# Three rearrangements in a two-layer transformer kernel: normalised softmax rows, a joined differential softmax, routing in channel order

## The chip, the cores and the metric

The kernel runs on one core of a Trainium2 chip. The time is device microseconds (us) of one execution, the median of several runs. Engines are called PE (matrix multiply), PEld (its weight load), DVE (vector), ACT (scalar), POOL and SP; DMA issues stand on ACT's or SP's queue.

## The reference, cut to what matters

256 tokens of width 1024 in float32 go through two layers of a first block and then two layers of a second block.

```python
# first block, per layer: attention of 8 GQA heads and 8 MLA heads
sc = jnp.einsum('bqhgd,bkhd->bhgqk', qblk, k).astype(jnp.float32) * scale
p = jax.nn.softmax(sc, axis=-1).astype(v.dtype)
return jnp.einsum('bhgqk,bkhd->bqhgd', p, v)
...
```

The second block modulates its two norms by a vector of a condition `c` (shift, scale and gate for each norm), mixes the tokens by a gated linear attention, a retention and a differential attention, and then sends each token to a few of 32 experts. The differential attention takes softmax(S0) - lam * softmax(S1) under a causal mask, multiplies by the values and applies a norm over each head's 128 outputs. The router computes logits = (norm(x) * g * (1 + scale) + shift) @ router_w, a sigmoid, and a group-limited choice of the top experts.

## The kernel before, in words

`first_layer(0)` and `first_layer(1)` run first, then `second_mix(0)`, `second_moe(0)`, `second_mix(1)`, `second_moe(1)`. Every engine runs its instructions in the order in which the program writes them. Weights come in 2 MB pieces through one list on SP's queue into eight slots; from a slot ACT copies a "granule" of 128x512 as the rounded high part (L257, `wh`) and DVE subtracts it to get the low part (L269, `wl`), a few granules ahead of PE, which multiplies high and low parts one after the other (all ordinary matmuls stand at L150).

**First-layer attention (`attention`, L680 to L720).** There are 16 units per layer of two (head, query tile) pairs each. One turn `i` of the loop issues: scores of unit i on PE; copies of finished transposes `PTs`; `soft` for unit i-1 (DVE row maximum L667, two ACT exponentials L670 that also give the row sums `su`); `soft_diag` for unit i-2 (L673: a DVE reciprocal, then two 128x128 diagonal matrices of it through `diag`, L428 to L431, one on DVE and one on POOL); `fill(i)`, which multiplies other weights' granules; and for unit i-3 four matmuls of P with the diagonal (L718), which turn and scale P at once. Each of them is two instructions on PE.

```python
                    mm(PT[h][:, o:o + 128], P[:, j, kt * 128:(kt + 1) * 128], dg[j], True, True)
```

**Differential attention (in `second_mix`).** Eight units (4 heads, 2 query tiles) per layer; tile 0 sees 128 keys, tile 1 sees 256. `d_soft` (L1532) makes two exponentials, `d_diag` (L1540) a reciprocal, a multiplication by -lam and two diagonals, and PE adds P0 diag(1/s0) and P1 diag(-lam/s1) into one bank for each key tile. `head_norm` (L1192) then takes the norm of each head.

**The modulation vector turned (`turn_mod`, L374).** The shift and scale of the second norm (columns 24:40 of `modc`, channel k*128+p on partition p) are needed with channel p*8+k on partition p (`modr`). ACT's queue writes them to a DRAM tensor `mod_turned`, element by element, at the start of `second_mix(0)` (L1243), between the loads of the constants `c` (L1226) and `GB` (L1242); they are read back behind the H projection (L1263). On ACT the squares of x (`sumsq`, L406) for the first norm of the mix come behind these issues; POOL makes the reciprocal root (L483, L414, L415), and ACT and DVE scale x (`DA`), which PE turns (L454).

**Routing (in `second_moe`, L1676 to L1783).** x is turned on PE with a stride of eight channels (`turn`, L1688), so that channel p*8+k lies on partition p; a bias matmul of the shift with `router` follows; the logits are made with the scaled router `ra` as the 32-column stationary operand in four column groups, copied by DVE (`lg`), summed over the groups and turned back by a matmul with `sumI`. `warm` then issues 20 matmuls whose result is not used. DVE adds the bias (`th`), ACT takes a tanh (L1734), a chain of some twenty DVE instructions picks experts, PE counts tokens (`sel`), and `place` multiplies one-hot rows `oh` with the normed tokens `xr`. The MoE follows, which streams expert weights.

Of the kernel before, what the change touches and what calls it, by code (L numbers as in the profile page):

```python
# [67 lines left out]
def constants():  # L68
# [20 lines left out]
    for lv in range(7):  # L89
# [27 lines left out]
       ("kv_a_norm_g", 2), ("b_gate", 16), ("norm1_g_2", 8), ("b_mod_2", 48),  # L117
# [17 lines left out]
def build(ctx, tc, I, out, cols, cols2, dbg=None):  # L135
# [537 lines left out]
    def soft_diag(P, su):  # L673
        r = small(2)
        dve.reciprocal(r, su)
        return P, [diag(r[:, j:j + 1], pool if j else dve) for j in range(2)]

    def attention(n, qk, heads_of, pair, vsrc, fill):


        Sb, PD, PT, full_, PS, cnt = {}, {}, {}, [], {}, {}
        for i in range(n + 4):
            if i < n:
                Sb[i] = qk(i)
# [12 lines left out]
            if 0 <= i - 2 < n:  # L697
                PD[i - 2] = soft_diag(*PD[i - 2])
# [12 lines left out]
            P, dg = PD.pop(u)  # L711
# [480 lines left out]
    def head_norm(src, g, e, gate, dest):  # L1192
# [3 lines left out]
        def squares():  # L1196
            sq, ss = t2((128, g * e), name="sq"), small(g)
            act.activation(sq, src, AF.Square)
            dve.tensor_reduce(ss, sq.rearrange("p (g e) -> p g e", e=e), axis=AX.X, op=OP.add)
            hold["r"] = rstd(ss, e)  # L1200
# [21 lines left out]
    def second_mix(l):  # L1222
# [4 lines left out]
        if l == 0:  # L1227
            turn_mod(False)
# [34 lines left out]
        if l == 0:  # L1263
            turn_mod(True)
# [32 lines left out]
        act.activation(GB[:, 512:1024], ob, AF.Copy)  # L1297

# [59 lines left out]
        for _ in proj("D1_%d" % l, qk_evac(0)):  # L1358
            pass

# [171 lines left out]
        def d_soft(v, n):  # L1532
            nm, su, r = small(2), small(2), small(2)
            dve.tensor_reduce(nm, v, axis=AX.X, op=OP.max, negate=True)
            P = t2((128, 2, 256), name="P")
            for j in range(2):
                act.activation(P[:, j, :n], v[:, j], AF.Exp, bias=nm[:, j:j + 1], accum_out=su[:, j:j + 1])
            return P, su, r

        def d_diag(P, su, r):  # L1540
            dve.reciprocal(r, su)
            dve.tensor_tensor(r[:, 1:2], r[:, 1:2], neglam[l], op=OP.mult)
            return P, [diag(r[:, j:j + 1], pool if j else dve) for j in range(2)]

        def d_norm(pr):
            return head_norm(oD.pop(0), 4, 128, gsub[l][:, None, None, :].to_broadcast([128, 2, 2, 128]),
                             mixed[:, :, 256 + pr * 256:512 + pr * 256])
        nu = len(units)
        turned = None
        for i in range(nu + 4):  # L1550
# [8 lines left out]
            if 0 <= i - 2 < nu:  # L1559
                PD[i - 2] = d_diag(*PD[i - 2])  # L1560
            if 0 <= i - 1 < nu:
                PD[i - 1] = d_soft(Sb.pop(i - 1), 128 * (units[i - 1][1] + 1))
# [21 lines left out]
            P, dg2 = PD.pop(i - 3)  # L1584
            if t == 0:
                AT[h] = bank()
            for kt in range(t + 1):
                b = AT[h][:, (kt + t) * 128:(kt + t + 1) * 128]
                for j in range(2):
                    mm(b, P[:, j, kt * 128:(kt + 1) * 128], dg2[j], j == 0, j == 1)  # L1590
# [31 lines left out]
        a2 = small(8, name="a2")  # L1622
        ra = t2((128, 8, NE), name="ra")
        dve.scalar_tensor_tensor(a2, modr[:, l, 1], 1.0, g2run[:, l], op0=OP.add, op1=OP.mult)
        pool.tensor_tensor(ra, router, a2[:, :, None].to_broadcast([128, 8, NE]), op=OP.mult)
# [51 lines left out]
    def second_moe(l):  # L1677
# [5 lines left out]
        def turn(k0, on_act):  # L1683
            p = bank()
            for k in (k0, k0 + 1):
                for t in range(2):
                    o = (k - k0) * 256 + t * 128
                    pe.transpose(p[:, o:o + 128], x[:, t, k::8], ident)  # L1688
# [3 lines left out]
            else:  # L1692
                dve.tensor_copy(xT[k0 // 2], v)
        steps[0]()
# [7 lines left out]
        dve.tensor_copy(rb, p[:, :NE])  # L1702
# [3 lines left out]
        turn(4, False)  # L1706
        turn(6, True)


        xr = [[wk.tile([128, 4, 128], F, name="xr", tag=("macc", "wh")[h], bufs=(NACC, NSPLIT)[h]) for h in range(2)] for t in range(2)]  # L1710
        for h in range(2):
            for t in range(2):
                act.activation(xr[t][h], x[:, t].rearrange("p (c k) -> p k c", k=8)[:, h * 4:h * 4 + 4], AF.Copy, scale=rx[:, t:t + 1])  # L1713
# [12 lines left out]
        for t in range(2):  # L1726
            mm(p[:, t * 32:(t + 1) * 32], lg[:, t * 128:(t + 1) * 128], sumI, t == 0, True)
# [6 lines left out]
        act.activation(th, th, AF.Tanh, scale=0.5)  # L1734
        dve.scalar_tensor_tensor(bi.rearrange("p (t e) -> p t e", t=2), th.rearrange("p (t e) -> p t e", t=2), 0.5,
# [333 lines left out]
```

## Time and profile before

| | before |
|---|---|
| median of 3 runs | 2126.85 us (2126.64 to 2130.85) |
| the profiled execution | 2126.68 us, span 2124.9 us |
| granted PE clock, mean | 0.976 of full speed |
| PE busy | 2024.3 us (95%) |
| DVE busy | 1011.0 us (48%) |
| ACT busy | 792.0 us (37%) |
| POOL busy | 247.9 us (12%) |

The span is the time from the first instruction to the last; the rest of the execution lies around it. A busy share is an average over stages with different limits, so a stage is read by its own stretch of time.

### The profile page before, as it was taken

To read this page: it belongs to the slowest core of one execution; us is meant where nothing else is said; L and a number is where in the kernel's file an instruction comes from. 1 tells how busy PE (TensorE), PEld (TensorE's weight loads), DVE (VectorE), ACT (ScalarE), POOL (GpSimd) and SP (SyncE) were. 2 spreads that over 40 slices of the span, in tenths; PEclk is the share of its full clock that TensorE was granted. 3 is DMA by queue.
4 is the path that set the end of the run, shared out by engine and by line. 5 is a ranking of instruction groups with operands and counts; after the bars stand their busy time and mean duration, and the time that the engine had idled before them with its cause. 6 is when DMAs were issued, how large, how long until landed. Compare 5 with 4: busy or idle time off the path is not lost. (4 is left out here: it accounts for less than half of the span.)

```text
span 2124.9 us, 29291 instructions
## 1 busy us (share of the span) xinstructions
PE 2024.3 (95%) x11522; PEld 1382.3 (65%) x11522; DVE 1011.0 (48%) x1901; ACT 792.0 (37%) x1605; POOL 247.9 (12%) x309
## 2 busy tenths in 40 slices
PE   8999999999999997999999889998999999969998
PEld 6888999788889986686444434446686444434443
DVE  4777877777778874875111111124875111101112
ACT  6655655566565555453111111114453111101111
POOL 1211000021100002621000000003531000000000
PEclk9999999999999998999999989999999999989999
DMA  6545777454558844446999999996256999979997
GB/s 232 212 160 198 279 280 276 170 191 149 206 212 316 308 158 80 157 185 248 417 428 427 426 370 428 427 417 237 81 186 240 419 427 427 428 297 429 426 427 309
DMA packets 135472, 620.92 MB, mean 292 GB/s; under 512 B 13594, under 2 KB 18724, under 8 KB 109220
## 3 DMA queue, kind: packets, MB, share of 16 engines
q1 hardware_dynamic: 129508, 614.78, 73.1%
q10 hardware_dynamic: 5824, 4.23, 1.1%
q8 instruction: 92, 1.51, 0.3%
q14 instruction: 48, 0.39, 0.1%
HBM read 617.93 MB, written 1.06 MB: 291 GB/s over the span
## 5 line engine op out<-in xcount | busy, mean ns | idle before, releaser
L150 PE MATMUL bank<-U,wh 128*128 128x256 f32 x1536 | 287.4, 288 | 0.5 <-DVE U L440 0.4
L150 PEld LDWEIGHTS bank<-U,wh 128*128 128x128 f32 x1536 | 239.8, 190 | 8.4 <-issue 5.3
L150 PE MATMUL bank<-w_eg,qwh 128*64 128x512 f32 x1024 | 228.1, 598 | 16.5 <-issue 16.5
L150 PE MATMUL bank<-w_ed,uT 128*64 128x512 f32 x1024 | 226.8, 595 | 0.3
L150 PE MATMUL bank<-w_eu,qwh 128*64 128x512 f32 x1024 | 226.7, 595 | 0.0
L150 PE MATMUL bank<-U,wl 128*128 128x256 f32 x768 | 218.4, 284 | 4.8 <-DVE wl L269 4.8
L1823 ACT ACTIVATE qwh<-bank,modr,a 128x128 f32<-128x128 f32 x128 | 58.6, 458 | 350.1 <-PE bank L150 319.2
L150 PEld LDWEIGHTS bank<-w_eg,qwh 128*64 128x64 f32 x1024 | 73.8, 138 | 163.8 <-issue 161.0
L150 PE MATMUL bank<-wh,H 128*128 128x512 f32 x512 | 163.8, 395 | 0.0
L150 PEld LDWEIGHTS bank<-w_eu,qwh 128*64 128x64 f32 x1024 | 70.8, 137 | 139.6 <-issue 138.7
L150 PE MATMUL bank<-wh,HT 128*128 128x512 f32 (+1 forms) x448 | 156.3, 403 | 0.6 <-ACT wh L257 0.6
L150 PEld LDWEIGHTS bank<-w_ed,uT 128*64 128x64 f32 x1024 | 70.7, 137 | 129.1 <-issue 127.3
L150 PEld LDWEIGHTS bank<-U,wl 128*128 128x128 f32 x768 | 145.9, 190 | 6.1 <-DVE wl L269 6.0
L150 PEld LDWEIGHTS bank<-oh,xr 128*128 128x128 f32 x1056 | 123.2, 192 | 26.0 <-issue 24.3
L150 PE MATMUL bank<-oh,xr 128*128 128x128 f32 (+1 forms) x1056 | 131.5, 278 | 1.2 <-DVE oh L1801 1.2
L596 DVE SCALAR_TENSOR_TENSOR macc<-w_mod,cact,macc 128x512 f32<-128x512 f32 x168 | 127.0, 756 | 0.0
L440 DVE SCALAR_TENSOR_TENSOR qwl<-bank,sm,qwl 128x512 fp32r<-128x512 f32 x60 | 45.0, 751 | 170.2 <-ACT qwl L439 166.2
L1803 POOL TENSOR_TENSOR ohg<-oh,wgt 128x256 f32<-128x256 f32 x32 | 19.7, 615 | 844.0 <-DVE oh L1801 844.0
L150 PEld LDWEIGHTS bank<-wh,H 128*128 128x128 f32 x512 | 96.5, 188 | 21.7
L257 ACT ACTIVATE wh<-w_dn 128x512 fp32r<-128x512 f32 x128 | 80.8, 631 | 74.7 <-PE bank L150 71.5
L1821 DVE TENSOR_SCALAR qwh<-bank,a,modr 128x128 f32<-128x128 f32 x128 | 52.4, 410 | 117.7 <-ACT qwh L1823 117.7
L257 ACT ACTIVATE wh<-w_up 128x512 fp32r<-128x512 f32 x128 | 80.3, 630 | 73.2 <-PE bank L150 66.6
(526 smaller groups left out, 3484.0 us busy)
## 6 DMA issues: line engine op xcount, KB each, us to landing
w_eg<-in_w_gate SPq DMA_DIRECT2D x60, 2048.0 KB
w_eu<-in_w_up SPq DMA_DIRECT2D x60, 2048.0 KB
w_ed<-in_w_down SPq DMA_DIRECT2D x60, 2048.0 KB
w_mod<-in_w_mod SPq DMA_DIRECT2D x24, 2048.0 KB
w_up<-in_w_ffn_up SPq DMA_DIRECT2D x16, 2048.0 KB
w_dn<-in_w_ffn_down SPq DMA_DIRECT2D x16, 2048.0 KB
w_gate<-in_w_in SPq DMA_DIRECT2D x8, 2048.0 KB
w_D<-in_w_in SPq DMA_DIRECT2D x6, 2048.0 KB
```

The lines of the kernel that those rows point to most:

```text
L150: pe.matmul(o, a, b, start=start, stop=stop, skip_group_check=True)
L257: act.activation(hi[:, :n], src, AF.Copy)
L440: dve.scalar_tensor_tensor(lo, src, scale, hi.bitcast(F), op0=OP.mult, op1=OP.subtract)
L596: dve.scalar_tensor_tensor(acc, w[:, k], cact[:, k:k + 1], acc, op0=OP.mult, op1=OP.add)
L1803: pool.tensor_tensor(og, oh, wg3[:, :, A][:, :, :, None].to_broadcast([128, 2, 2, 64]), op=OP.mult)
L1821: dve.tensor_scalar(hg[k], o, a2[:, k:k + 1], b2[:, k:k + 1], op0=OP.mult, op1=OP.add)
L1823: act.activation(hg[k], o, AF.Identity, scale=a2[:, k:k + 1], bias=b2[:, k:k + 1])
```

## The change

1. In the first-layer attention the rows of P are multiplied by their reciprocal sums in place: the first of a unit's pair on DVE (128x256), the second on ACT (128x256). PE then only turns P, one transpose per 128x128 tile. The diagonals on DVE and POOL go.
2. In the differential attention `d_join` forms P0 - lam (s0/s1) P1 in one DVE instruction, and PE turns one tile instead of adding two products. The missing factor 1/s0 is taken up by the norm: `head_norm` gets the sums s0 and multiplies its epsilon by their square, which takes five small POOL instructions instead of two.
3. `turn_mod` turns the columns on PE, copies the 16 rows on ACT and writes rows of 512 bytes. The write moves behind the G projection, the read-back behind the first D projection.
4. Routing uses channels in natural order: x is turned from contiguous columns, the bias matmul takes the shift straight from `modc`, and the logits come directly as tokens x 32 experts (turned x stationary, `ra` moving, 32 columns), so `lg` and the sum over groups go. `router` is loaded in pieces of 128 bytes instead of 1 KB; one small DVE instruction (`an`) and one more vector load (`norm2_g_2`) come in. The four `xr` copies move behind the tanh.

```diff
-            else:
-                act.dma_start(turned_[l].rearrange("s (k p) -> p s k", p=128), modc[l][:, 24:40].rearrange("p (s k) -> p s k", s=2))
+                continue
+            p = bank()
+            pe.transpose(p[:16, :128], modc[l][:, 24:40], ident)
+            row = wk.tile([16, 128], F, name="mrow", tag="dg", bufs=6)
+            act.activation(row, p[:16, :128], AF.Copy)
+            act.dma_start(turned_[l].rearrange("s (k p) -> (s k) p", p=128), row)
...
-    def soft_diag(P, su):
+    def soft_norm(P, su):
         r = small(2)
         dve.reciprocal(r, su)
-        return P, [diag(r[:, j:j + 1], pool if j else dve) for j in range(2)]
+        dve.tensor_scalar(P[:, 0], P[:, 0], r[:, 0:1], None, op0=OP.mult)
+        act.activation(P[:, 1], P[:, 1], AF.Copy, scale=r[:, 1:2])
+        return P
...
-                    mm(PT[h][:, o:o + 128], P[:, j, kt * 128:(kt + 1) * 128], dg[j], True, True)
+                    pe.transpose(PT[h][:, o:o + 128], P[:, j, kt * 128:(kt + 1) * 128], ident)
...
-        nc.sync.dma_start(router, rows_of(I["router_w_2"]))
+        nc.sync.dma_start(router, kp(I["router_w_2"]))
...
+            ee, r = small(g), small(g)
+            pool.tensor_tensor(ee, over, over, op=OP.mult)
+            pool.tensor_scalar(ee, ee, EPS, None, op0=OP.mult)
+            pool.tensor_scalar(r, ss, 1.0 / e, None, op0=OP.mult)
+            pool.tensor_tensor(r, r, ee, op=OP.add)
+            pool.tensor_tensor(r, r, mhalf[:, :g], op=OP.pow)
...
-        def d_diag(P, su, r):
-            dve.reciprocal(r, su)
-            dve.tensor_tensor(r[:, 1:2], r[:, 1:2], neglam[l], op=OP.mult)
-            return P, [diag(r[:, j:j + 1], pool if j else dve) for j in range(2)]
+        def d_join(P, su0, su1, n):
+            r = small(1)
+            dve.reciprocal(r, su1)
+            dve.scalar_tensor_tensor(r, r, neglam[l], su0, op0=OP.mult, op1=OP.mult)
+            dve.scalar_tensor_tensor(P[:, 0, :n], P[:, 1, :n], r, P[:, 0, :n], op0=OP.mult, op1=OP.add)
+            return P
...
-                for j in range(2):
-                    mm(b, P[:, j, kt * 128:(kt + 1) * 128], dg2[j], j == 0, j == 1)
+                pe.transpose(b, P[:, 0, kt * 128:(kt + 1) * 128], ident)
...
-                    pe.transpose(p[:, o:o + 128], x[:, t, k::8], ident)
+                    pe.transpose(p[:, o:o + 128], x_chunk(t, k), ident)
...
+        def logits(k):
+            for t in range(2):
+                mm(lo_[:, t * 32:(t + 1) * 32], xT[k // 2][:, k % 2, t * 128:(t + 1) * 128], ra[:, k], k == 0 and t == 0, k == 7)
...
-            mm(p[:, :NE], b2[:, k:k + 1].to_broadcast([128, 128]), router[:, k], k == 0, k == 7)
+            mm(p[:, :NE], ms(3)[:, k:k + 1].to_broadcast([128, 128]), router[:, k], k == 0, k == 7)
...
-        p = bank()
-        for k in range(8):
-            c = (k % 4) * 32
-            mm(p[c:c + 32, :256], ra[:, k], xT[k // 2][:, k % 2], k < 4, k >= 4)
-        lg = t2((128, 256), name="lg")
-        dve.tensor_copy(lg, p[:, :256])
-        p = bank()
-        for t in range(2):
-            mm(p[:, t * 32:(t + 1) * 32], lg[:, t * 128:(t + 1) * 128], sumI, t == 0, True)
+        p = lo_
         warm(WARM)
```

Three places show how the instructions move; the rows are the programs' own order on one engine.

ACT, around the start of `second_mix(0)`, before: the loads of the constants `c` and `GB`, the two writes of `mod_turned`, and the squares of x (into `junk`).

```order
L257 ACTIVATE wh<-w_H_8219 128x272 x3
L406 ACTIVATE junk,sm<-bank 128x512 x2
L1226 DMA c_8572<-in_cst 128x2182
L380 DMA mod_turned<-modc_82 128x16x1
L380 DMA mod_turned<-modc_83 128x16x1
L1242 DMA GB<-in_m 128x896
L406 ACTIVATE junk,sm<-x 128x512 x4
L257 ACTIVATE wh<-w_H_8219 128x272
L505 ACTIVATE DA<-x,sm 128x512 x2
```

ACT behind the G projection, changed:

```order
L257 ACTIVATE wh<-w_D_0_8476 128x512 x3
L1309 ACTIVATE GB<-bank 128x256
L1311 ACTIVATE GB<-bank 128x512
L383 ACTIVATE mrow<-bank 16x128
L384 DMA mod_turned<-mrow 16x128
L383 ACTIVATE mrow<-bank 16x128
L384 DMA mod_turned<-mrow 16x128
L1322 ACTIVATE ab<-zt 128x256
```

Nothing stands any more between the load of `c` and that of `GB`, and so before the squares of x; two small copies and two writes stand behind the evacuation of G.

ACT in the middle of the first layer's attention, before (`w_ba` is the weight of branch a, `A` and `PTs` are copies of banks):

```order
L257 ACTIVATE wh<-w_ba_1178 128x512
L670 ACTIVATE P,sm<-bank,sm 128x256 x2
L934 ACTIVATE A_1444<-bank 96x512
L689 ACTIVATE PTs<-bank 128x512
L257 ACTIVATE wh<-w_ba_1178 128x512
L670 ACTIVATE P,sm<-bank,sm 128x256 x2
```

The same stretch, changed:

```order
L257 ACTIVATE wh<-w_ba_1176 128x512
L674 ACTIVATE P,sm<-bank,sm 128x256 x2
L682 ACTIVATE P<-P,sm 128x256
L941 ACTIVATE A_1432<-bank 96x512
L696 ACTIVATE PTs<-bank 128x512
L257 ACTIVATE wh<-w_ba_1176 128x512
L674 ACTIVATE P,sm<-bank,sm 128x256 x2
```

One multiplication of a 128x256 tile stands behind each pair of exponentials.

PE in the routing, before, from the last matmul of the out-projection to the placing:

```order
L150 MATMUL bank<-wh,MT 128x512
L1688 MATMUL bank<-C,x 128x128 x8
L150 MATMUL bank<-router,modr 128x32 x8
L1688 MATMUL bank<-C,x 128x128 x8
L150 MATMUL bank<-xT,ra 32x256 x8
L150 MATMUL bank<-C,lg 128x32 x2
L150 MATMUL bank<-C 128x128 x20
L150 MATMUL bank<-sel,C 128x64
```

And changed:

```order
L150 MATMUL bank<-wh,MT 128x512
L1712 MATMUL bank<-C,x 128x128 x8
L150 MATMUL bank<-router,modc_82 128x32 x8
L150 MATMUL bank<-ra,xT 128x32 x8
L1712 MATMUL bank<-C,x 128x128 x8
L150 MATMUL bank<-ra,xT 128x32 x8
L150 MATMUL bank<-C 128x128 x20
L150 MATMUL bank<-sel,C 128x64
```

Half of the logits now stand between the two groups of transposes, and the step over `lg` is gone.

## Rows read from the trace of the kernel before

**Rows 1.** The page, busy time of each engine over the span.
```profile
PE 2024.3 (95%) x11522; PEld 1382.3 (65%) x11522; DVE 1011.0 (48%) x1901; ACT 792.0 (37%) x1605; POOL 247.9 (12%) x309
```
**Rows 2.** Windows: stretch, length, then PE, PEld, DVE, ACT, POOL busy; clock; DMA share; GB/s.
```profile
91.00:153.00 62.00, 62.00 (x456) 53.64 (x456) 43.38 (x91) 37.30 (x107) 10.33 (x14) 1.00 0.44 158
488.00:551.00 63.00, 63.00 (x474) 55.23 (x472) 44.21 (x96) 36.02 (x104) 10.80 (x15) 1.00 0.38 134
1550.00:1570.00 20.00, 19.84 (x99) 15.13 (x98) 18.40 (x49) 9.78 (x34) 5.60 (x7) 1.00 0.08 28
```
**Rows 3.** Timeline of PE, first layer: start, length, instruction, count; [idle before].
```profile
83.54 1.03 PE L908 MATMUL bank<-C,T 128*128 128x128 f32 x8
...
106.93 1.05 PE L150 MATMUL bank<-dg,P 128*128 128x128 f32 x8
107.82 1.02 PE L150 MATMUL bank<-kbd,M 128*128 128x512 f32 x2
```
**Rows 4.** Groups of instructions: count, busy us, mean ns of one, idle before.
```profile
L150 PE MATMUL bank<-dg,P 128*128 128x128 f32 x352 | 48.1, 278 | 0.0
L430 DVE TENSOR_SCALAR dg<-C,sm 128x128 f32<-128x128 f32 x48 | 13.6, 283 | 1.1
L437 DVE TENSOR_TENSOR Y<-bank,Y 128x256 fp32r<-128x256 f32 x16 | 6.6, 424 | 17.3 <-ACT Y L436 17.1
L470 ACT ACTIVATE HT<-h 128x256 fp32r<-128x256 f32 x16 | 5.7, 405 | 0.0
L667 DVE TENSOR_REDUCE sm<-bank 128x2 f32<-128x512 f32 x32 | 21.8, 681 | 0.0
```
**Rows 5.** Timeline, start of the second block's first mix (ACTq is ACT's queue).
```profile
792.22 6.93 ACTq L380 DMA_DIRECT2D mod_turned<-modc  x1
...
793.86 2.74 DVE L557 SCALAR_TENSOR_TENSOR x<-ag,sm,x 128x512 f32<-128x512 f32 x4 [1.18 <-POOL sm L553]
...
799.18 4.27 ACTq L1242 DMA_DIRECT2D GB<-in_m  x1
...
806.61 0.19 POOL L483 TENSOR_TENSOR sm<-sm 128x2 f32<-128x2 f32 x1 [12.78 <-ACT junk L406]
...
808.67 1.97 PE L454 MATMUL bank<-C,DA 128*128 128x128 f32 x8 [15.85 <-ACT DA L505]
```
**Rows 6.** DMA view of 799 to 806 us: queue, packets, MB, share of 16 engines.
```profile
q10 hardware_dynamic: 3698, 0.04, 81.6%
```
**Rows 7.** Timeline, start of the second block's second mix.
```profile
1448.85 0.37 ACTq L1242 DMA_DIRECT2D GB<-in_m  x1
1449.55 2.47 DVE L1862 TENSOR_TENSOR x<-x,bank 128x512 f32<-128x512 f32 x4
...
1453.33 0.19 POOL L483 TENSOR_TENSOR sm<-sm 128x2 f32<-128x2 f32 x1 [17.35 <-ACT junk L406]
```
**Rows 8.** Timeline, routing of the first second-block layer.
```profile
959.92 3.00 POOL L1638 TENSOR_TENSOR x<-x,pn 128x512 f32<-128x512 f32 x2 [10.42 <-DVE pn L1637]
...
962.85 0.40 PE L150 MATMUL bank<-wh,MT 128*128 128x512 f32 x1
...
966.34 3.02 PE L150 MATMUL bank<-router,modr 128*128 128x32 f32 x16
...
969.17 1.95 PE L1688 MATMUL bank<-C,x 128*128 128x128 f32 x8
...
974.03 4.71 PE L150 MATMUL bank<-C 128*128 128x128 f32 x40
...
976.10 0.25 ACT L1734 ACTIVATE th<-th 128x64 f32<-128x64 f32 x1
...
980.55 1.05 PE L150 MATMUL bank<-sel,C 128*128 128x64 f32 x8 [1.81 <-DVE sel L1771]
```
**Rows 9.** Windows of both routings, columns as in rows 2.
```profile
967.00:973.50 6.50, 5.98 (x36) 4.40 (x35) 1.31 (x3) 3.85 (x8) 1.09 (x3) 0.50 1.01 429
...
1615.40:1625.60 10.20, 9.65 (x53) 8.07 (x53) 3.00 (x14) 6.46 (x10) 1.38 (x4) 0.50 0.66 280
```
**Rows 10.** Timeline, the unused matmuls in the second routing.
```profile
1622.10 6.37 PE L150 MATMUL bank<-C 128*128 128x128 f32 x40
```

More of the change, by code (lines that the diff above doesn't have):

```diff
@@ L1199, in squares @@
             dve.tensor_reduce(ss, sq.rearrange("p (g e) -> p g e", e=e), axis=AX.X, op=OP.add)
-            hold["r"] = rstd(ss, e)
+            if over is None:
+                hold["r"] = rstd(ss, e)
+                return
+            ee, r = small(g), small(g)
[4 more added lines that the diff above has]
+            pool.tensor_tensor(r, r, mhalf[:, :g], op=OP.pow)
+            hold["r"] = r
         def norm():
@@ L1359, in second_mix @@
             pass
+        if l == 0:
+            turn_mod(True)
         GA = slot("GA", [128, 4096])
@@ L1530, in d_scores, with d_soft @@
             return v
-        def d_soft(v, n):
-            nm, su, r = small(2), small(2), small(2)
+        def d_soft(v, n, first_sum):
+            nm, su = small(2), small(1)
             dve.tensor_reduce(nm, v, axis=AX.X, op=OP.max, negate=True)
             P = t2((128, 2, 256), name="P")
-            for j in range(2):
-                act.activation(P[:, j, :n], v[:, j], AF.Exp, bias=nm[:, j:j + 1], accum_out=su[:, j:j + 1])
-            return P, su, r
-        def d_diag(P, su, r):
-            dve.reciprocal(r, su)
-            dve.tensor_tensor(r[:, 1:2], r[:, 1:2], neglam[l], op=OP.mult)
-            return P, [diag(r[:, j:j + 1], pool if j else dve) for j in range(2)]
+            for j, s_ in enumerate((first_sum, su)):
+                act.activation(P[:, j, :n], v[:, j], AF.Exp, bias=nm[:, j:j + 1], accum_out=s_)
+            return P, first_sum, su, n
+        def d_join(P, su0, su1, n):
[4 more added lines that the diff above has]
+            return P
         def d_norm(pr):
             return head_norm(oD.pop(0), 4, 128, gsub[l][:, None, None, :].to_broadcast([128, 2, 2, 128]),
-                             mixed[:, :, 256 + pr * 256:512 + pr * 256])
+                             mixed[:, :, 256 + pr * 256:512 + pr * 256], sums[pr])
         nu = len(units)
+        sums = [small(4) for _ in range(2)]
         turned = None
@@ L1559, in second_mix @@
             if 0 <= i - 2 < nu:
-                PD[i - 2] = d_diag(*PD[i - 2])
+                PD[i - 2] = d_join(*PD[i - 2])
             if 0 <= i - 1 < nu:
-                PD[i - 1] = d_soft(Sb.pop(i - 1), 128 * (units[i - 1][1] + 1))
+                h1, t1 = units[i - 1]
+                j1 = t1 * 2 + h1 % 2
+                PD[i - 1] = d_soft(Sb.pop(i - 1), 128 * (t1 + 1), sums[h1 // 2][:, j1:j1 + 1])
             if i in RET_T:
@@ L1621, in second_mix @@
         g1 = bcast_row(ms(2))
-        a2 = small(8, name="a2")
+        a2, an = small(8, name="a2"), small(8, name="an")
         ra = t2((128, 8, NE), name="ra")
         dve.scalar_tensor_tensor(a2, modr[:, l, 1], 1.0, g2run[:, l], op0=OP.add, op1=OP.mult)
-        pool.tensor_tensor(ra, router, a2[:, :, None].to_broadcast([128, 8, NE]), op=OP.mult)
+        dve.scalar_tensor_tensor(an, ms(4), 1.0, V(l, "norm2_g_2"), op0=OP.add, op1=OP.mult)
+        pool.tensor_tensor(ra, router, an[:, :, None].to_broadcast([128, 8, NE]), op=OP.mult)
         route_ahead[l] = (a2, modr[:, l, 0], ra)
@@ L1693, in turn @@
                 dve.tensor_copy(xT[k0 // 2], v)
+        lo_ = bank()
+        def logits(k):
+            for t in range(2):
+                mm(lo_[:, t * 32:(t + 1) * 32], xT[k // 2][:, k % 2, t * 128:(t + 1) * 128], ra[:, k], k == 0 and t == 0, k == 7)
         steps[0]()
@@ L1699, in second_moe @@
         for k in range(8):
-            mm(p[:, :NE], b2[:, k:k + 1].to_broadcast([128, 128]), router[:, k], k == 0, k == 7)
+            mm(p[:, :NE], ms(3)[:, k:k + 1].to_broadcast([128, 128]), router[:, k], k == 0, k == 7)
         rb = small(32, name="rb")
-        dve.tensor_copy(rb, p[:, :NE])
+        for k in range(4):
+            logits(k)
+        turn(4, False)
+        turn(6, False)
         steps[2]()
@@ L1705, in second_moe @@
         rx = steps[4]()
[L1706 to L1711, printed above, removed]
-            for t in range(2):
-                act.activation(xr[t][h], x[:, t].rearrange("p (c k) -> p k c", k=8)[:, h * 4:h * 4 + 4], AF.Copy, scale=rx[:, t:t + 1])
+        for k in range(4, 8):
+            logits(k)
+        dve.tensor_copy(rb, p[:, :NE])
         def quarter(tag, dt=F):
             return wk.tile([128, 512], dt, name="q" + tag, tag=tag, bufs=NSPLIT)
-        p = bank()
-        for k in range(8):
-            c = (k % 4) * 32
-            mm(p[c:c + 32, :256], ra[:, k], xT[k // 2][:, k % 2], k < 4, k >= 4)
-        lg = t2((128, 256), name="lg")
-        dve.tensor_copy(lg, p[:, :256])
-        p = bank()
-        for t in range(2):
-            mm(p[:, t * 32:(t + 1) * 32], lg[:, t * 128:(t + 1) * 128], sumI, t == 0, True)
+        p = lo_
         warm(WARM)
@@ L1734, in second_moe @@
         act.activation(th, th, AF.Tanh, scale=0.5)
+        xr = [[wk.tile([128, 4, 128], F, name="xr", tag=("macc", "wh")[h], bufs=(NACC, NSPLIT)[h]) for h in range(2)] for t in range(2)]
+        for h in range(2):
+            for t in range(2):
+                act.activation(xr[t][h], x[:, t].rearrange("p (c k) -> p k c", k=8)[:, h * 4:h * 4 + 4], AF.Copy, scale=rx[:, t:t + 1])
         dve.scalar_tensor_tensor(bi.rearrange("p (t e) -> p t e", t=2), th.rearrange("p (t e) -> p t e", t=2), 0.5,
```

17 lines of the change are left out of this document (7 added, 10 removed).

## Prediction

> **What bounds the kernel now.** The page's first part comes first [rows 1]: PE is busy 95% of the span and no other engine over half of it. That share is a mean over stages, so the windows view is read next for the stages that the change touches [rows 2]. In both layers' attention PE is busy for all of the 62 and 63 us, while DVE has 43 to 44 us of work and ACT 36 to 37: PE sets the pace, and an instruction taken from it shortens the stage as long as the others stay under it. In the differential attention PE has 19.84 us of 20, but DVE has 18.40: PE leads by little. Two places are read from the timeline instead, since PE stands still there: the start of the second block, where PE idles 15.85 us [rows 5], and the routing, where a chain through DVE and ACT sets the end [rows 8].
>
> **First-layer attention.** Eight PE instructions of the diagonal product hold PE from 106.93 to 107.82, 0.111 us each [rows 3]. (The group's mean of 278 ns [rows 4] contains the overlap with the next instruction and is not used.) A row of eight transposes lasts 1.03 us against 1.05 [rows 3], so a transpose costs the same 0.111 us, but is one instruction where the product was two. A unit has four tiles: 8 x 0.111 - 4 x 0.111 = 0.44 us less, and 32 units give 14.2 us. What comes in lies on other engines. DVE gives up a 128x128 diagonal of 0.283 us and takes a 128x256 multiplication, bounded by 0.283 and twice that; its nearest row is 0.424 for another 128x256 operation, with two tensor inputs. That is at most 0.28 us per unit, 4.5 us per layer if at its dearest. ACT takes a 128x256 copy with a scale, 0.405 us by the nearest row, 6.5 us per layer [rows 4]. PE's 62 us shrink by some 7, to 55, with ACT at about 44 and DVE at 45 to 48: both still fit under it. On average the cover is thinner than before, and the turn's two ends are not average: ACT's multiplication waits for DVE's reciprocal, which stands behind a row maximum of 0.681 us. I take **-13**, with -7 (half swallowed) and -14.2 as bounds, -13 being near the end that the windows' free time speaks for. POOL's diagonals go as well; they were not on the path.
>
> **Differential attention.** Before, 96 PE instructions over both layers (352 of that group less 32 x 8 in the first block) cost 96 x 0.111 = 10.7 us; now 24 transposes cost 2.7. That is 8.0 us less on PE. DVE gets no lighter: the small multiplication and the 0.283 us diagonal give way to a small instruction and one of 128 or 256 columns, up to 0.424. With DVE at 18.40 of 20 us [rows 2], PE can give back little more than 1.4 us of such a stretch before DVE leads, and two such stretches per layer stand against 4.0 us. Between them I take **-6**, bounds -3 and -8. The norm behind it has one more link on its path (the two on the sums alone can run before): the step between two small POOL starts is about 0.3 us by my estimate from POOL's 0.19 us instruction [rows 5] with its wait, so **+0.6** for two layers, bounds 0 and +1.2.
>
> **Start of the second block.** Here x is done at 796.60 (793.86 + 2.74), yet POOL gets the squares' sums only at 806.61, 10.01 us later; ACT's queue is held 6.93 us by the second write of the modulation and 4.27 us by the load behind it [rows 5]. In the second layer's mix, without the writes, that load takes 0.37 us to issue, x is done at 1452.02 and POOL starts at 1453.33, 1.31 us later [rows 7]. The difference, 8.7 us, is what the two writes cost; PE has nothing else there. In the stretch from 799 to 806 the queue with these writes made 3698 packets for 0.04 MB and took 81.6% of the DMA engines' time [rows 6]. The Trainium skill ("DMA: Bandwidth & Descriptors", Rules for kernel authors) says that a last dimension that isn't contiguous becomes one descriptor per element; the packets of the trace agree, 11 bytes each. Behind G come two transposes, two copies of 16x128 (under 0.405 us each) and two issues (0.37 each), under 1.6 us on ACT beside PE's projection: I charge 0.5. So **-8.2**, bounds 0 (the wait moves behind G) and -8.7. The read-back has the whole of D1 and the attention before `a2` needs it.
>
> **Routing.** The last out-projection matmul ends at 963.25; the tanh starts at 976.10 and the count of tokens at 980.55 [rows 8]. The clock is the question: from 967 to 973.5 it was 0.50, the lower level (1.2 GHz), and in the second layer 0.50 for 10.2 us [rows 9]. At that level the 16 bias instructions took 3.02 us, 0.19 each, and 8 transposes 1.95 [rows 8]; the logits now have the bias's form, 32 instructions. The first two turns read only the first 512 columns of x, which POOL finishes at 962.92, so they start at once. Then at the lower level: turns 1.0 (still fast), bias 3.0, half of the logits 3.0, turns 2.0, two DVE copies of 128x512 at the 0.681 of another such bank read [rows 4], 1.4, logits 3.0: 976.7; half of these logits need only the first copy, so about 975.5. The bias addition follows, and the tanh starts at about 976.0, as before. At the higher level every PE term halves: turns 0.9, bias 1.8, logits 1.8, turns 0.9, copies 0.9, logits 1.8, to 971.3; tanh at 971.8, 4.3 us earlier. The unused matmuls stand ahead of the count: 4.71 us, or 6.37 in the slow stretch of the second layer [rows 8, 10]; with logits at 975.5 they end between 980.2 and 981.9, so the count could be 1.3 us later than now. PE has fewer holes than before between 963 and 967, which should hold the clock a little longer, so I take -1 per layer, **-2**, with bounds +2.6 and -8.6. The Trainium skill ("TensorE: Matmul & The Clock Gate", Part 4) says that transposes don't count as PE work for the clock in the way matmuls do, which speaks against a routing that begins with them; by it the lower level stays, which is what I forecast, and no row here separates the transposes from the gaps around them.
>
> **Small things.** The four `xr` copies behind the tanh run beside DVE's chain of 4.45 us (976.10 to 980.55 [rows 8]) and the placing starts behind the count, so they are taken as nothing. The router in 128-byte pieces is loaded at the start of the kernel among constants; 0 to +1 us, taken as nothing. Ahead of the routing the DMA engines stand at a share of 0.08 [rows 2], with nothing to fill, so what is gained ahead of the MoE is carried to the end.
>
> **Sum.** -13 - 6 + 0.6 - 8.2 - 2 = -28.6 us on the profiled 2126.68, which is 0.17 below the median of 2126.85: **2098 us**.
>
> **Rivals.**
> - *The clock holds in the routing.* For it: PE is fed without a gap from 963.25. Against: it was at 0.50 for most of this work in both layers [rows 9]. Then -8.6 replaces -2: 2091.5 us.
> - *DVE and ACT set the pace of the attentions.* For it: DVE's 18.40 of 20 us, and the new link from DVE's reciprocal to ACT and on to PE [rows 2]. Against: a third of ACT's and DVE's time is free in the first-layer stretches. Half of the PE savings arrive, -7 and -3: 2107 us.
> - *The start of the second block keeps its gap* (the change doesn't do there what it says): another transfer on ACT's queue, `c` or `GB`, holds the squares. For it: `GB` too took 4.27 us [rows 5]. Against: 0.37 in the other layer [rows 7]. Without the 8.2: 2106 us.
> - *Slower: ACT stalls in every unit.* ACT's multiplication of unit i-2 waits for the reciprocal behind DVE's row maximum and a low part, and ACT's granule copies for PE are queued behind it. The price is 32 times the stall; from 0.9 us per unit it eats the whole 28.6. A stall of a maximum and a multiplication (0.681 + 0.424 [rows 4]) gives 35: 2133 us. Against: the reciprocal's sums are a whole turn old, and 16 units share some 62 us, nearly 4 us each.
>
> **How the numbers follow.** The forecast has a chance of 0.5 with its own range 2093 to 2103; the clock that holds 0.17; half savings 0.22; the gap that stays 0.06; the stall 0.03; and 0.02 for a change that ends within 0.2% (about 4 us, what a measurement can tell from none). If all terms fell to one end together, the sum would be -39.5 or -6.2, each less likely than any case above; the range takes the cases without the stall, and some us on either side: **2086 to 2111 us**. Faster by over 0.2%: 0.95; within: 0.02; slower: 0.03.
>
> **What would show it.** In the profile after: the group of products with a diagonal gone, PE's part of the first-layer stretches shorter by some 7 us per layer, DVE and ACT still under it (right), or PE with idle time before transposes or granules, released by DVE or ACT (the second rival). At the start of the second block POOL's sum about 1.3 us behind x, and the writes' issue short. In the routing the granted clock, the length of the unused matmuls and the distance from the last out-projection matmul to the count, 17.3 us before. The prediction is wrong if the first block's share of the gain is under 7 us, or if the second block's stages grow.

## The result

The changed kernel takes 2104.05 us (median of 4 runs, 2103.31 to 2105.73), the kernel before 2126.74 (4 runs): a ratio of 0.9892, 95% interval 0.988 to 0.9905, so about 23 us less (20 to 25.5). That is faster, inside the range, 6 us short of the forecast of 2098. The profiled execution took 2105.73 us, its span 2103.9.

The page of the changed kernel, busy time of each engine, against [rows 1]:

```profile
PE 2010.9 (96%) x11348; PEld 1368.0 (65%) x11348; DVE 1014.5 (48%) x1903; ACT 803.3 (38%) x1637; POOL 218.5 (10%) x273
```

PE has 13.4 us less to do, ACT 11.3 more, POOL 29.4 less. Where the time went is read from the starts of the same instructions in both timelines (the first row ends at ACT's first copy of an FFN granule in the second layer of the first block; a routing begins with the last out-projection matmul):

| from, to | before | after | difference |
|---|---|---|---|
| first product with P, to the first FFN granule of the second layer | 486.7 | 475.1 | -11.6 |
| to PE's first turn of x in the second block | 219.7 | 211.5 | -8.2 |
| first mix, to the last out-projection matmul | 154.2 | 155.7 | +1.5 |
| first routing, to the first expert's matmul | 23.6 | 20.9 | -2.7 |
| first MoE, to PE's first turn of x in the second mix | 469.3 | 469.7 | +0.4 |
| second mix | 155.2 | 155.5 | +0.3 |
| second routing | 23.3 | 22.5 | -0.8 |
| second MoE, to the last instruction | 490.6 | 490.7 | +0.1 |

The rows add up to -21.0, the difference of the two spans.

**First-layer attention.** Timeline of PE (start, length, instruction, count; in brackets idle time and who ended it), against [rows 3], and a row some 30 us later:

```profile
106.44 0.60 PE L725 MATMUL bank<-C,P 128*128 128x128 f32 x4
106.88 1.02 PE L150 MATMUL bank<-kbd,M 128*128 128x512 f32 x2
...
140.31 1.08 PE L150 MATMUL bank<-PTs,Z 128*64 128x256 f32 x6 [0.67 <-ACT PTs L696]
```

The four transposes hold PE 0.44 us (106.44 to 106.88), the eight instructions before held it 0.89: the saving of a unit is the predicted one. The third row is new: PE waits for the copy of the turned tiles on ACT. Summed over the stretch from the first to the last product with P (each instruction counted up to the start of the next), the tiles cost PE 7.5 us less in each layer, and the products with `PTs` 1.9 us more: 0.67 of it is this one wait, 1.2 that the products stretch. The windows (columns as in [rows 2]) show how much thinner the cover is:

```profile
91.00:147.00 56.00, 55.33 (x398) 47.23 (x397) 42.26 (x89) 40.05 (x114) 0.00 (x0) 1.00 0.48 175
...
1529.00:1549.00 20.00, 17.44 (x77) 12.45 (x75) 18.61 (x45) 8.46 (x29) 2.96 (x4) 1.00 0.10 39
```

ACT has 40.05 us of work in 56, where it had 37.30 in 62. The groups name the new instructions' prices, 505 ns on ACT and 353 on DVE, and 419 for the join:

```profile
L682 ACT ACTIVATE P<-P,sm 128x256 f32<-128x256 f32 x32 | 16.2, 505 | 0.7 <-DVE sm L680 0.7
...
L681 DVE TENSOR_SCALAR P<-P,sm 128x256 f32<-128x256 f32 x32 | 11.3, 353 | 1.1
...
L1563 DVE SCALAR_TENSOR_TENSOR P<-P,sm 128x128 f32<-128x128 f32 (+1 forms) x16 | 6.7, 419 | 0.6
```

**Differential attention.** In the second of the windows above PE is down from 19.84 to 17.44 us, but DVE is busy 18.61 of 20. The whole stretch, from the start of the first product with P to the end of the last one, stands in the next windows: both layers of the changed kernel, then the second layer of the kernel before (the first is equal to it):

```profile
890.70:914.01 23.31, 20.41 (x95) 14.84 (x93) 20.27 (x49) 12.03 (x37) 4.42 (x7) 0.93 0.30 110
1537.54:1560.15 22.61, 19.22 (x95) 13.82 (x93) 20.30 (x49) 11.90 (x37) 4.43 (x7) 1.00 0.33 118
...
1558.13:1580.99 22.86, 22.70 (x131) 18.08 (x129) 19.89 (x50) 11.30 (x35) 7.41 (x10) 1.00 0.35 122
```

The stretch is as long as it was, 23.3 and 22.6 us against 22.9. PE, which had 0.2 us of idle time in it, now has 2.9 and 3.4. In the first layer the granted clock also fell to the lower level behind PE's longest wait, which the mean of 0.93 shows; in the second, with the same wait, it did not, and the difference is 0.7 us. In the kernels with the joined tile that ran, the clock fell in 14 of 18 such stretches, in those with the diagonals in none of 10. PE's new waits, from its timeline:

```profile
1544.07 0.91 PE L150 MATMUL bank<-DA,aT 128*128 128x128 f32 x6 [1.95 <-DVE sm L1561]
...
1546.12 0.63 PE L1523 MATMUL bank<-C,rt 128*128 128x128 f32 x4 [0.61 <-ACT P L1555]
...
1549.88 0.63 PE L1523 MATMUL bank<-C,rt 128*128 128x128 f32 x4 [0.66 <-DVE bank L1547]
```

**Start of the second block.** Timeline, against [rows 5]:

```profile
780.76 0.47 ACTq L1258 DMA_DIRECT2D GB<-in_m  x1
...
782.90 2.74 DVE L561 SCALAR_TENSOR_TENSOR x<-ag,sm,x 128x512 f32<-128x512 f32 x4 [1.19 <-POOL sm L557]
...
786.81 0.19 POOL L487 TENSOR_TENSOR sm<-sm 128x2 f32<-128x2 f32 x1 [3.94 <-ACT junk L410]
788.87 1.54 PE L458 MATMUL bank<-C,DA 128*128 128x128 f32 x6 [7.01 <-ACT DA L509]
```

x is done at 785.64 and POOL starts 1.17 us later, 10.01 before; PE's idle time at its first turn is 7.0 us instead of 15.85.

**Routing.** Timeline of the first layer, against [rows 8]:

```profile
944.54 0.39 PE L150 MATMUL bank<-wh,MT 128*128 128x512 f32 x1
...
945.64 1.87 PE L150 MATMUL bank<-router,modc 128*128 128x32 f32 x16
...
947.34 1.95 PE L150 MATMUL bank<-ra,xT 128*128 128x32 f32 x16
...
950.55 3.62 PE L150 MATMUL bank<-ra,xT 128*128 128x32 f32 x16
...
953.98 5.95 PE L150 MATMUL bank<-C 128*128 128x128 f32 x40
954.27 0.41 DVE L1753 SCALAR_TENSOR_TENSOR th<-bank,sm,rb 128x32 f32<-128x32 f32 x2 [2.96 <-PE bank L150]
954.72 0.26 ACT L1754 ACTIVATE th<-th 128x64 f32<-128x64 f32 x1 [6.87 <-DVE th L1753]
...
959.77 0.98 PE L150 MATMUL bank<-sel,C 128*128 128x64 f32 x8
```

The first half of the logits takes 1.95 us, the second 3.62: the clock has fallen. The unused matmuls take 5.95 and end at the token count (L150 `sel`), which therefore starts 5.05 us behind the tanh instead of 4.45. The windows:

```profile
944.50:948.50 4.00, 4.00 (x37) 3.87 (x35) 2.45 (x4) 3.14 (x8) 0.49 (x4) 1.00 1.00 356
948.50:955.00 6.50, 6.45 (x37) 6.04 (x37) 1.89 (x5) 0.28 (x2) 0.69 (x1) 0.60 0.99 411
```

PE was busy without a gap ahead of this fall, with transposes and 32-column matmuls.

### The profile page after: what moved, and what is told of

Same layout as the page of the kernel before. It is cut to its first block, busy times and chain, and to the rows that moved or that the text cites. A ratio compares the mean times of both kernels' runs of the same rounds, so it can differ in the third digit from the quotient of the medians.

```text
span 2103.9 us, 28881 instructions
## 1 busy us (share of the span) xinstructions
PE 2010.9 (96%) x11348; PEld 1368.0 (65%) x11348; DVE 1014.5 (48%) x1903; ACT 803.3 (38%) x1637; POOL 218.5 (10%) x273
## 5 line engine op out<-in xcount | busy, mean ns | idle before, releaser
L150 PE MATMUL bank<-U,wh 128*128 128x256 f32 x1536 | 288.0, 289 | 0.3
L150 PEld LDWEIGHTS bank<-U,wh 128*128 128x128 f32 x1536 | 240.2, 190 | 8.2 <-issue 5.0
L150 PE MATMUL bank<-w_eg,qwh 128*64 128x512 f32 x1024 | 228.2, 599 | 16.7 <-DMA w_ed<-in_w_down 16.3
L150 PE MATMUL bank<-w_ed,uT 128*64 128x512 f32 x1024 | 226.8, 595 | 0.3
L150 PE MATMUL bank<-w_eu,qwh 128*64 128x512 f32 x1024 | 226.7, 595 | 0.0
L150 PE MATMUL bank<-U,wl 128*128 128x256 f32 x768 | 218.7, 285 | 4.8 <-DVE wl L269 4.7
L150 PEld LDWEIGHTS bank<-w_eg,qwh 128*64 128x64 f32 x1024 | 73.8, 138 | 164.1 <-issue 161.2
L150 PE MATMUL bank<-wh,H 128*128 128x512 f32 x512 | 163.9, 395 | 0.0
L150 PEld LDWEIGHTS bank<-w_eu,qwh 128*64 128x64 f32 x1024 | 70.8, 137 | 139.6 <-issue 138.6
L150 PE MATMUL bank<-wh,HT 128*128 128x512 f32 (+1 forms) x448 | 156.9, 404 | 0.6 <-ACT wh L257 0.6
L150 PEld LDWEIGHTS bank<-w_ed,uT 128*64 128x64 f32 x1024 | 70.7, 137 | 129.1 <-issue 127.3
L150 PEld LDWEIGHTS bank<-U,wl 128*128 128x128 f32 x768 | 146.0, 190 | 6.1 <-DVE wl L269 6.0
L150 PEld LDWEIGHTS bank<-oh,xr 128*128 128x128 f32 x1056 | 123.1, 192 | 25.8 <-issue 24.3
L150 PE MATMUL bank<-oh,xr 128*128 128x128 f32 (+1 forms) x1056 | 131.4, 278 | 0.9 <-DVE oh L1826 0.8
L150 PEld LDWEIGHTS bank<-wh,H 128*128 128x128 f32 x512 | 96.5, 188 | 21.7
```

Of the source, the lines that this page charges most:

```text
L150: pe.matmul(o, a, b, start=start, stop=stop, skip_group_check=True)
```

## The experiments

**Each part alone on the kernel before.** Four kernels take one part of the diff each: the normalised rows (`soft_norm` and its transposes), `turn_mod` with its two new places, `d_join` with the norm's epsilon, and the routing with the router's load. Here and below, a ratio is against runs of the kernel before that were made beside it.

```diff
+        dve.tensor_scalar(P[:, 0], P[:, 0], r[:, 0:1], None, op0=OP.mult)
+        act.activation(P[:, 1], P[:, 1], AF.Copy, scale=r[:, 1:2])
```

> The kernel before with the first-layer attention alone changed (rows of P multiplied by the reciprocal sums, transposes in place of the diagonal product). Theory A (PE gives up 7.1 and 7.5 us in the two layers, and about 1.9 us of each comes back as PE waiting for the PTs copies): 11 to 12 us less than before, about 0.9945 of it. Theory B (the sum of the prediction, nearly all of the 14.2 arrives): 13 us less or more.

```diff
+            act.dma_start(turned_[l].rearrange("s (k p) -> (s k) p", p=128), row)
```

> The kernel before with the turning of the modulation alone changed (rows of 512 bytes, written behind the G projection, read back behind D1). Theory A (the element writes cost only the wait at the start of the second block): 8.2 us less, POOL's first sum of that mix about 1.3 us behind x. Rival (the writes' wait moves behind G): the gain is below 5 us, and PE idles behind the G projection.

```diff
+            dve.scalar_tensor_tensor(P[:, 0, :n], P[:, 1, :n], r, P[:, 0, :n], op0=OP.mult, op1=OP.add)
```

> The kernel before with the differential attention alone changed (one joined tile, one transpose for each key tile, the sums in the norm's epsilon). Theory A (DVE sets the pace there, and the join is a dearer DVE instruction than the diagonal): 0 to 2 us slower than before, PE with some 4 us of idle time per layer in that stretch, released by DVE. Theory B (PE sets the pace, as the prediction had it in part): 6 us faster.

```diff
+                mm(lo_[:, t * 32:(t + 1) * 32], xT[k // 2][:, k % 2, t * 128:(t + 1) * 128], ra[:, k], k == 0 and t == 0, k == 7)
```

> The kernel before with the routing alone changed (natural channel order, logits straight, the router's load in small pieces). Theory A (the clock falls to the lower level in the second half of the logits and the unused matmuls hold the token count): 2 to 4 us faster in all. Rival (the whole chain is shorter by the tanh's advance): 4 to 9 us faster. Rival (the router's load in 128-byte pieces delays the first weights): a later start of the first projection, up to 1 us lost.

Measured against 2128.15 us of the kernel before in these runs:

| part | median | ratio (95%) | us |
|---|---|---|---|
| normalised rows | 2116.67 | 0.9948 (0.9933 to 0.9962) | -11.1 |
| modulation by rows | 2120.09 | 0.9957 (0.9944 to 0.997) | -9.1 |
| joined differential softmax | 2128.31 | 1.0003 (0.9994 to 1.0012) | +0.6 |
| routing | 2121.91 | 0.9965 (0.9952 to 0.9978) | -7.4 |

The four add up to -27.0, the whole measured -22.7; each part's interval reaches 2 to 3 us to either side, which covers the difference of 4 us. Three of the six runs of the normalised rows took 2113 us and three 2120 to 2121, so their median lies between two groups; by the timeline, PE's first turn of x in the second block comes 11.7 us earlier behind the first product with P, which supports the -11.1.

The first three came out as theory A had it; PE's idle time in the joined stretch was 3.4 and 2.9 us of the 4 expected. The routing came out as the second theory, more than the profiles of before and after show together (-3.5). Of the third, the first product with P starts at 101.8 to 102.3 us in the five kernels with the old load of the router and at 101.8 to 103.8 in the nine with the new one: some 0.6 us on the mean, which stays open. The two layers of the routing's one profiled execution say why it gained more. First come the windows of the second half of the logits in each (the clock stands third from the end), then the timeline of the unused matmuls and the count:

```profile
967.80:974.50 6.70, 6.70 (x33) 6.37 (x33) 1.66 (x5) 0.00 (x0) 0.67 (x1) 0.52 1.01 426
...
1614.40:1619.00 4.60, 4.25 (x38) 4.01 (x38) 1.79 (x5) 0.06 (x1) 0.67 (x1) 1.00 0.98 410
```
```profile
974.03 6.75 PE L150 MATMUL bank<-C 128*128 128x128 f32 x40
...
980.62 0.98 PE L150 MATMUL bank<-sel,C 128*128 128x64 f32 x8
...
1618.23 4.71 PE L150 MATMUL bank<-C 128*128 128x128 f32 x40
1623.42 1.05 PE L150 MATMUL bank<-sel,C 128*128 128x64 f32 x8 [0.47 <-DVE sel L1773]
```

The same instructions ran once at the lower and once at the higher level. From the out-projection's last matmul to the first expert's, the new routing took about 18.9, 21.0 or 22.5 us in the eight routings of the changed kernel, of this one and of the next two runs (mean 21.2); the old one 23.3 to 26.1 in the ten routings of the kernels that have it (mean 24.5, and 23.6 and 23.3 in the profile that the prediction read). Some 3.3 us per layer, 6.6 in all, fit the -7.4.

**The second multiplication on POOL** (on the changed kernel, as all that follow but one):

```diff
-        act.activation(P[:, 1], P[:, 1], AF.Copy, scale=r[:, 1:2])
+        pool.tensor_scalar(P[:, 1], P[:, 1], r[:, 1:2], None, op0=OP.mult)
```

> The changed kernel with the second multiplication of each unit's pair on POOL instead of ACT. Theory A (ACT, in order, reaches the PTs copies late because of its multiplications and granules, and PE waits for them 1.9 us per layer): the PTs waits shrink, 2 to 4 us less than the changed kernel (0.987 to 0.988 of the kernel before). Theory B (the PTs copies are late for want of time between the transposes and their use, whoever scales): no change, or slower if POOL's instruction comes late.

2101.89 us, 0.9873 (0.9853 to 0.9893), where the changed kernel has 0.9892; the intervals overlap, so the timeline has to tell. The wait for `PTs` is down from the 0.67 above:

```profile
139.70 1.08 PE L150 MATMUL bank<-PTs,Z 128*64 128x256 f32 x6 [0.27 <-ACT PTs L696]
```

The products with `PTs` cost PE 7.7 us in the first layer instead of 9.1, and the stretch from the first to the last product with P 52.0 and 52.9 us instead of 53.5 and 54.3. Theory A: ACT's order held the copies, by 1.4 of the 1.9 us per layer; the other 0.5 stays. An instruction on POOL takes 1105 ns here, and PE does not wait for it.

**Copies from DVE to ACT in the differential attention**, on the changed kernel and on the one before:

```diff
-                (act.activation(a, src, AF.Copy) if h % 2 else dve.tensor_copy(a, src))
+                act.activation(a, src, AF.Copy)
...
-            dve.tensor_copy(rqbd[0:64, :, 0, tk], p4[0:64, 0:2])
+            act.activation(rqbd[0:64, :, 0, tk], p4[0:64, 0:2], AF.Copy)
```

> The changed kernel with two pairs of copies in the differential attention moved from DVE to ACT (the aT copies of even heads and the retention's key copies; 1.9 us of DVE per layer). Theory A (DVE sets the pace of that stretch in the changed kernel): the stretch from the first to the last transpose of P is shorter by 1 to 1.9 us per layer, 2 to 4 us in all. Theory B (the longer chain of one unit, not DVE's load, sets the pace): under 1 us.

> The kernel before with the same copies in the differential attention moved from DVE to ACT as in the run on the changed kernel (which took 0.7 us per layer off that stretch). Theory A (PE sets the pace there in the kernel before, DVE only in the changed one): the stretch from the first to the last product of P stays at 21.8 us in both layers, no change in the total. Rival (DVE leads in both): it is shorter by 0.5 us or more per layer.

On the changed kernel: 2098.74 us, 0.9867 (0.9842 to 0.9892), the stretch, measured as above to the end of the last transpose, 22.6 and 22.0 us instead of 23.3 and 22.6, 0.7 less in each. On the kernel before: 1.0005 (0.9995 to 1.0014), the stretch 22.7 in both layers against 22.9 (the 21.8 of the expectation ends where the last row of products starts). So DVE's load helps to pace the changed kernel and hardly the one before. But DVE is busy 1.3 to 1.4 us less in the stretch and only 0.7 arrive, less than theory A expected and within theory B's limit: load and chain both count. The two stretches are also only 1.4 of the 5.3 us by which the medians differ. In the profiled executions the rest stands in a first routing of 18.9 instead of 20.9 us and in the two MoE stages, which this edit does not touch; the intervals meet. The longest of PE's waits stays and has only another name:

```profile
1540.35 0.94 PE L150 MATMUL bank<-DA,aT 128*128 128x128 f32 x6 [1.88 <-ACT aT L1579]
```

The copy on ACT stands behind exponentials that wait for DVE's maximum. What is left would then be the order of the chain; no run here changed it, so that is not shown.

**Routing: narrow work, wide work, unused work.** The bias matmul early, 8 instead of 20 unused matmuls, and four wide unused ones among the narrow:

```diff
+        p = bank()
+        for k in range(8):
+            mm(p[:, :NE], ms(3)[:, k:k + 1].to_broadcast([128, 128]), router[:, k], k == 0, k == 7)
...
         route_ahead[l] = (a2, modr[:, l, 0], ra, rb)
```

> The changed kernel with the bias matmul of the routing (16 narrow instructions) moved ahead of the last parts of the out-projection. Theory A (the clock falls after a stretch of narrow instructions and transposes on PE, gaps or not): with fewer of them in a row the clock holds for more of the logits; the count comes 2 to 4 us earlier after the out-projection's end, of which up to 1.8 per layer are given back in the out-projection. Theory B (the fall is set by something else, as the two levels in one and the same program suggest): the clock is 0.5 to 0.6 in the second half as before, and the time stays within 2 us.

```diff
-WARM = 20
+WARM = 8
```

> The changed kernel with 8 instead of 20 unused matmuls in the routing. Theory A (in the changed kernel they hold the token count by 0.7 and 1.4 us): 1 to 2 us less, the count 4.4 us behind the tanh in both layers. Rival (without them the clock stays low through the placing and the first expert): equal or slower, the placing's 32 instructions longer than 3.81 us.

```diff
+            for _ in range(n):
+                mm(w, ident, xT[0].rearrange("p k q -> p (k q)"), True, True)
...
+        wide(2)
         for k in range(4):
             logits(k)
+        wide(2)
```

> The changed kernel with four unused 128x512 matmuls (1.85 us of PE per routing by the 0.46 us of one in the attention) among the narrow ones: two behind the bias, two behind the first half of the logits. Theory A (what counts for the clock is how wide the work of that stretch is): granted clock 1.0 through the logits in both layers, the last logits 1.8 instead of 3.6 us, the count about 15 us behind the out-projection's end in both layers (15.3 and 16.8 in the changed kernel), so 0 to 2 us faster. Theory B (the level in this stretch is a matter of chance in one execution): one or both layers fall to 0.5 or 0.6 as before, and each costs 1.8 us more.

With the bias early: 2102.99 us, 0.988 (0.9861 to 0.99), no difference that can be told. The clock stayed at 1.00 through the logits of both layers and the count came 11.7 us behind the start of the out-projection's last matmul (15.2 and 16.8 in the changed kernel), but that matmul is 1.7 and 3.2 us later behind PE's first turn of x, and in the second layer the clock fell one step further on, in the placing, whose 32 instructions took 5.44 us instead of 3.81.

With 8 unused matmuls: 2108.92 us, 0.9905 (0.9883 to 0.9928), not faster. The count starts 4.5 us behind the tanh in both layers, as theory A had it, but the rival decides. Timeline of the first layer:

```profile
958.87 1.89 PE L150 MATMUL bank<-sel,C 128*128 128x64 f32 x8 [1.45 <-DVE sel L1796]
960.77 6.41 PE L150 MATMUL bank<-oh,xr 128*128 128x128 f32 x32
```

In both layers the placing takes longer than the 3.81 us it has behind 20 unused matmuls: 6.41 and 6.66.

With the wide ones: 2106.81 us, 0.9906 (0.9889 to 0.9923), no gain, and the count 16.5 us behind that matmul, not 15. One of them holds PE for 0.86 us, two instructions 0.43 apart, and not the 0.46 of the expectation. That price was misread: the two instructions of the attention's 128x512 product start 0.43 apart too, and its row above (106.88) lasts 1.02 us. But the clock is the one of theory A, in both layers and down to the first expert:

```profile
949.00:955.00 6.00, 5.66 (x39) 4.41 (x39) 1.39 (x3) 0.00 (x0) 0.00 (x0) 1.00 0.98 418
955.00:966.00 11.00, 9.94 (x88) 9.70 (x87) 6.15 (x30) 6.13 (x9) 0.90 (x2) 1.00 0.02 6
...
1597.00:1603.00 6.00, 5.65 (x39) 4.41 (x39) 1.39 (x3) 0.00 (x0) 0.00 (x0) 1.00 0.95 396
```

These are two occurrences of one execution, and the routing without the wide ones kept the clock in two of eight. The mean granted clock of all four executions speaks for theory A as well, though not by itself: 0.980 to 0.981 with the wide ones, 0.976 to 0.978 in the changed kernel, up to 0.982 in one execution of the kernel with the moved copies.

**Three edits together, and with wide unused matmuls.**

```diff
-        warm(WARM)
+        wide(10)
```

> The changed kernel with three edits that each made it faster or equal alone: second multiplication on POOL, two pairs of copies from DVE to ACT, bias matmul of the routing early. If the parts add up: 5 to 8 us less than the changed kernel, 0.9855 of the kernel before (0.984 to 0.987). If ACT, which gets the copies and loses the multiplication in different stages, or the clock in the placing takes something back: 2 to 5 us.

> The kernel with the three edits, and in place of the 20 unused 128x128 matmuls of the routing 10 of 128x512, about the same length on PE at the higher level. Theory A (wide work keeps the clock where narrow work doesn't): the placing at granted clock 1.0 in both layers, its 32 instructions 3.8 us, where the kernel with the early bias alone took 5.44 us in its second layer; 0 to 2 us less than with the narrow ones. Theory B: the level in the placing differs from layer to layer all the same, no difference in the total.

The three edits together: 2099.48 us, 0.9868 (0.9852 to 0.9885), by the medians some 5 us below the changed kernel, with intervals that just overlap, and the fastest but one of all that ran (the copies alone reached 2098.74, within its interval); it is the second of the two cases expected, and that the parts add up is not shown. Its routing reaches the count 11.7 us behind the start of the out-projection's last matmul in both layers, and pays in the placing, 5.44 us in each:

```profile
957.49 5.44 PE L150 MATMUL bank<-oh,xr 128*128 128x128 f32 x32 [0.65 <-DVE oh L1826]
```

With the wide ones behind it (first row, 20 instructions for the ten) the placing is back at its length, in both layers:

```profile
950.02 8.83 PE L150 MATMUL bank<-xT,C 128*128 128x512 f32 x20
...
960.09 3.81 PE L150 MATMUL bank<-oh,xr 128*128 128x128 f32 x32 [0.42 <-DVE oh L1831]
```

But ten of them last 8.83 us instead of 4.7 and hold the count: 2103.88 us, 0.9888 (0.9872 to 0.9905). By these rows five would be about as long as the narrow ones, an estimate; that wasn't tried.

## Why the prediction was right, and where it was not

- **First-layer attention, -13.** Measured -11.1 alone and -11.6 in the stages. The PE saving of 14.2 was right to within a microsecond (15.0 by the rows). What was mis-sized is the part swallowed: 3.7 us and not 1.2. The run with POOL shows that ACT's order, at 505 ns per multiplication where the sum had 405, is most of it (2.9 of 3.7). POOL, left free, was the better place for it.
- **Differential attention, -6 + 0.6.** This step failed: +0.6, with an interval of about -1.3 to +2.6. The sum took DVE's free time, 1.4 us of 20, twice per layer, as time that PE could give back (the stretch of 22.9 us had 3.0 of it), and chose a value between this and the full saving; its bounds excluded a loss for no reason. In the changed kernel the stretch ends no sooner although DVE still has 2.3 us of it idle: PE's saving of 3.9 us per layer turned into waits behind DVE and ACT, and with them the clock fell in one layer. A join of 419 ns in place of a diagonal of 283 made DVE heavier as well. How much is DVE's load and how much the order of one unit's chain is open: taking load off gave back 0.7 us per layer. Behind the stretch another 0.6 us per layer were lost, which the sum had priced at 0.3 for the longer link of the norm: from the end of the last product with P to the start of the out-projection's last matmul it is 30.4 us before and 30.9 after, in both layers. But the link is not the reason: in the second layer POOL ends it at 1558.11 us, and DVE, never idle in between, comes to its result at 1559.76. PE then waits for what DVE makes of it (`MX`):

```profile
1562.11 0.63 PE L1443 MATMUL bank<-C,MX 128*128 128x128 f32 x4 [0.39 <-DVE MX L1227]
```

- **Start of the second block, -8.2.** Right: -8.2 in the stages, -9.1 alone (-7.6 by that run's own timeline). The writes behind G cost about the half microsecond that was charged: from PE's first turn of x to the first product with P in that mix it is 101.4 us before and 101.8 after.
- **Routing, -2.** Mis-sized: -7.4 alone, -3.5 between the two profiles. The mechanism (a fall of the clock in the logits, then the unused matmuls holding the count) is what the profile of the changed kernel shows, but forecast and first rival are not alternatives: both happen, layer by layer, in one program. And the old routing's price came from one execution, which was among its shortest.
- **The total.** Between the two profiles nearly the whole miss is the differential attention. That the total lies inside the stated range owes something to its width: 2104 is just outside the forecast's own 2093 to 2103 and nearer to the second rival's 2107. That rival, in which DVE and ACT set the pace of the attentions, was half of the truth: it held in the differential attention, where nothing arrived, and only for a quarter of the saving in the first layers. Of the signs of being wrong one came in part: the two mixes of the second block grew, by 1.5 and 0.3 us. The slower case did not come: PE's waits for the copies are 0.12 us per unit (1.9 of 16 units), far from 0.9.

## What to carry over

- Before a saving on one engine is counted, add the new work to the engine next behind it in that very stretch. What that engine seems to have free may be waits in the chain of one unit: here DVE, busy 19.9 of 22.9 us, got heavier, and the saving was zero.
- New work goes where the order of a queue hurts no one: here an idle engine with an instruction twice as long did better, by 1.4 us of PE's time per layer, than a faster one whose later instructions are waited for.
- Price a stage whose clock changes level from several executions, and look at each of its occurrences: one profile shows one draw.

## What was not expected of the hardware

- PE's granted clock fell to 0.5 or 0.6 behind 4 us in which PE was busy without a gap, with transposes and 32-column matmuls, in some occurrences of the same code and not in others. With four 128x512 matmuls among them it stayed at 1.00 in both layers. The Trainium skill ("TensorE: Matmul & The Clock Gate", Part 4) sets transposes apart from other PE work for the clock; the fall came here behind work that begins with transposes, but the runs do not tell them from 32-column matmuls.
- A DVE instruction on one column took 1.00 us instead of some 0.2 while POOL added two 128x512 tiles, and ended with it, at each of the four such additions, in the changed kernel as in the one before (0.95 to 1.02 there). In the changed kernel DVE then has no idle time up to the copy for which PE waits 1.95 us, so these 0.8 us are part of that wait:

```profile
1539.66 1.27 POOL L1413 TENSOR_TENSOR rt<-rt,rb 128x512 f32<-128x512 f32 x1 [11.87 <-DVE rt L1412]
1539.76 0.15 DVE L1561 RECIPROCAL sm<-sm 128x1 f32<-128x1 f32 x1
1539.95 1.00 DVE L1562 SCALAR_TENSOR_TENSOR sm<-sm,neglam 128x1 f32<-128x1 f32 x1
```
